# Differential attention: PV sums moved into spare columns of a lasting score tile, one PSUM bank handed to the projections, and one minimum taken by a single reduce

## The chip, the core and the metric

The kernel runs on one core of one Trainium2 chip. The metric is the device time of one execution in microseconds (us), as a median of several runs. Five engines work side by side and wait for each other through semaphores: TensorE (PE, matrix multiplies, whose weight loads are shown apart as PEld), VectorE (DVE), ScalarE (ACT), GpSimd (POOL) and SyncE (SP), which issues most of the DMAs. Each engine takes its instructions in the order in which they stand.

## What is computed

A block of two layers works on 2048 latent tokens and 256 context tokens of width 1024. Each layer normalises the tokens, multiplies them with one wide projection matrix, feeds four groups of heads from it (differential attention, HGRN2, windowed attention, mLSTM), gates their joined output, and projects it back. The change lies in differential attention, which has four heads:

```python
def attend(qs, ks, vs):                      # qs, ks: two maps (m) per head, 32 wide; vs: 64 wide
    s = jnp.einsum('mbhqd,mbhkd->mbhqk', qs, ks).astype(F32) * scale
    p = jax.nn.softmax(s, axis=-1)
    w = (p[0] - lam * p[1]).astype(vs.dtype)
    return jnp.einsum('bhqk,bhkv->bhqv', w, vs)
...
y = from_heads(rmsnorm(o, g) * (1.0 - lam_init))
```

Each query row has two maps of scores against all 2304 keys. Both are turned into softmax weights, the second is subtracted with the factor lam, and the difference is multiplied with the values ("PV" below).

## The kernel before

In each layer there is first a stage that normalises and transposes the tokens and makes the projections that differential attention needs. Then comes the **diff loop**, in which differential attention runs while all the other projections are worked off in its gaps. After it the windowed attention, mLSTM, HGRN2 and output streams are woven together.

The diff loop walks over **units**. A unit is one head and one tile of 128 queries: 64 units with latent queries in each layer, and 8 with context queries in layer 0 alone. For a latent unit the 2304 keys are cut into two halves (HALF): 1024 keys and 1280 keys. Keys are in fp16 as a high and a low part, and so are the values and the weights. For a unit u the steps are these:

- diff_scores(u, m) makes the scores of one map. PE writes the first half into the tile sc0 (1024 columns, two matmuls of 512), then works off some projections (`pump(FSTEP)`), then writes the second half into sc1 (1536 columns reserved, 1280 used, three matmuls). DVE takes a minimum over each half (L1048). A last small instruction joins the two minima into the bias of the exponential: L1054, a tensor_tensor, for map 1, and L1056, a tensor_scalar, for map 0.
- diff_exp(u, m) is the exponential of each half on ACT, read straight from sc0 and sc1.
- diff_mix(u, j) subtracts the maps on DVE (L1082), splits the difference into two fp16 parts on ACT (L1084) and POOL (L1085), and has a DMA transpose it into wt (L1087).
- diff_out(u, j) is PV of half j on PE. For each block of 128 keys there are two matmuls: the high weights with the high and low part of the values (128 columns) and the low weights with the high part (64 columns). Both halves add up in one tile pv.
- diff_norm(u, 0) copies one half of pv, scaled, to ot on ACT, and diff_norm(u, 1) adds the other half to it on DVE (oall, L1120).

Four units are in flight: while u makes scores, u1, u2 and u3 are the three before it. The order of one round is written out by hand, and it is PE's order word for word; the other engines' order is set by a scheduler at build time:

```python
diff_scores(u, 1); diff_out(u3, 1); pump(FGAP); diff_mix(u1, 0); diff_exp(u, 1); diff_norm(u3, 0)
diff_scores(u, 0); diff_norm(u3, 1); diff_out(u2, 0); pump(FGAP); diff_mix(u1, 1); diff_exp(u, 0)
```

So on PE a PV burst stands right behind the three matmuls of sc1, and projections (`pump(FGAP)`) stand behind the burst. A round has two such **map steps**: sc0, projections, sc1, a PV burst, projections.

The matmuls' output memory, PSUM, is dealt out in pools that add up to eight banks of 512 fp32 columns: in the diff loop two for sc0, three for sc1, one for pv and two for the projections (pool pps, tag "pp"). After the diff loop, while projections are left, windowed attention has three, mLSTM three (function bank, GPB = 4) and the projections two; when they are done, bank also draws from a second pool.

The tiles' waits are placed by the framework that builds the program, from what each instruction reads and writes. The small tile sm holds a unit's minima, sums and biases; u["nm"] is the joining instruction behind which diff_mix is issued. All matmuls but the transposes are recorded in a helper at L94, the activations at L105, the tensor_tensor operations at L108 and the fused DVE operations at L111.

Of the kernel before, what the change touches and what calls it, by code (L numbers as in the profile page):

```python
# [10 lines left out]
F32 = mybir.dt.float32  # L11
# [3 lines left out]
AF = mybir.ActivationFunctionType  # L15
ALU = mybir.AluOpType
# [57 lines left out]
def kernel(  # L74
# [29 lines left out]
    def act(o, i, f, **kw):  # L104
        A.activation(out=o, in_=i, func=f, **kw)  # L105

    def tt(e, o, a, b, op):
        return e.tensor_tensor(out=o, in0=a, in1=b, op=op)  # L108
# [150 lines left out]
    for l in range(n_layers):  # L259
# [79 lines left out]
            hl[g] = hp.tile([P, KC, GROUPS[g][1]], F16, tag=f"hl{g}", name=f"hl{l}_{g}")  # L339
        wst = ExitStack()  # L340
        wp = wst.enter_context(tc.tile_pool(name=f"wp{l}", bufs=1, reuse_waits="tile"))
        pps = wst.enter_context(tc.tile_pool(name=f"pps{l}", bufs=2, reuse_waits="tile", space=PSUM))
        with tc.tile_pool(name=f"pa{l}", bufs=2, reuse_waits="tile", side="right" if l else "left") as pa, tc.tile_pool(name=f"pap{l}", bufs=4, space=PSUM, reuse_waits="tile") as pap:
            xgs = {}

# [682 lines left out]
        with ExitStack() as st2:  # L1028
            da = st2.enter_context(tc.tile_pool(name=f"da{l}", bufs=2, reuse_waits="tile", side="right"))
            sps = st2.enter_context(tc.tile_pool(name=f"sps{l}", bufs=1, reuse_waits="tile", space=PSUM, side="right"))  # L1030
            HALF = [(0, 1024), (1024, 1280)]

            def halves_of(u):
                return [(2048, 256)] if u["ctx"] else HALF

            def diff_scores(u, m):


                sm, hs = u["sm"], halves_of(u)
                pss = u["s", m] = []  # L1040
                for j, (k0, n) in enumerate(hs):
                    ps = sps.tile([P, 1536 if j else 1024], F32, tag=f"sc{j}", name="scr")
                    for o in range(0, n, 512):
                        w = min(512, n - o)
                        mm(ps[:, o:o + w], u["Qs"][:, m, u["qo"]:u["qo"] + P], u["Ks"][m][:, k0 + o:k0 + o + w], True, True)
                    if j < len(hs) - 1:
                        pump(FSTEP * u["work"])
                    V.tensor_reduce(sm[:, m * 2 + j:m * 2 + j + 1], ps[:, :n], AX.X, ALU.min)  # L1048
                    pss.append(ps)
                o = m * 2  # L1050
                o2 = o + len(hs) - 1

                if m:
                    u["nm"] = tt(V, sm[:, 5:6], sm[:, o:o + 1], sm[:, o2:o2 + 1], ALU.min)  # L1054
                else:
                    u["nm"] = V.tensor_scalar(sm[:, 4:5], sm[:, o:o + 1], sm[:, o2:o2 + 1], shf, ALU.min, ALU.add)  # L1056

# [32 lines left out]
            def diff_out(u, j):  # L1090

                sm, hs = u["sm"], halves_of(u)
                if j >= len(hs):
                    return
                if u["start"]:
                    h = u["h"]
                    k0_, n_ = HALF[j]
                    head["V", j] = da.tile([P, n_ // P, P], F16, tag=f"Vs{j}", name=f"Vs{h}", bufs=1)
                    SP.dma_start(head["V", j], dva[k0_:k0_ + n_, h].rearrange("(t p) c -> p t c", p=P))
                if j == 0:  # L1100
                    u["pv"] = sps.tile([P, 512], F32, tag="pv", name="pv")
                pv, wt = u["pv"], u["w"][j]
                nb = hs[j][1] // P
                vv = head["V", 1][:, 8:] if u["ctx"] else head["V", j]
                fin = j == len(hs) - 1
                for b in range(nb):
                    mm(pv[:, 0:P], wt[:, b], vv[:, b], j == 0 and b == 0, False)
                    mm(pv[:, 0:64], wt[:, nb + b], vv[:, b, 0:64], False, fin and b == nb - 1)

            def diff_norm(u, j):  # L1110
                sm, pv = u["sm"], u["pv"]
                if j == 0:
                    ot = u["ot"] = da.tile([P, 64], F32, tag="ot", name="ot")
                    act(ot, pv[:, 64:128], AF.Copy, scale=sm[:, 12:13])
                    return
                ot, (i, nq) = u["ot"], u["of"]
                if i == 0:
                    head["o"] = da.tile([P, 8, 64], F32, tag="oall", name="oall")
                oall = head["o"]
                stt(oall[:, i], pv[:, 0:64], sm[:, 12:13], ot, ALU.mult, ALU.add)  # L1120
                if i == nq - 1:
                    h, q0 = u["h"], u["qt"] + 1 - nq
                    rs = da.tile([P, 2, 8], F32, tag="rs", name=f"drs{h}")
# [9 lines left out]
            def units():  # L1133
                for h in range(4):
# [5 lines left out]
                    for g in ([0, 1, 4, 2, 3] if cq else [0, 1, 2, 3]):  # L1140
# [5 lines left out]
                        for i in range(n // P):  # L1146
                            qt = g0 // P + i
                            ctx_ = qt >= NL
                            yield dict(h=h, qt=qt, Ks=Ks, Qs=Qs, qo=i * P, ctx=ctx_, start=qt == 0,
                                       work=CTXW if ctx_ else 1.0, of=(i, 2) if ctx_ else (qt % 8, 8),  # L1150
                                       sm=da.tile([P, 16], F32, tag="sm", name="sm", bufs=5))

            owed = [0.0]

            def pump(ns):
                owed[0] += ns
# [42 lines left out]
        with ExitStack() as st4:  # L1201
# [10 lines left out]

            def bank(shape, name):
                turn_[0] += 1
                if gps2 and turn_[0] % GPB == 0:
                    return gps2.tile(shape, F32, tag="gp", name=name)
                return gps.tile(shape, F32, tag="gp", name=name, bufs=GPB - 1)

            def yt_of(i):

# [506 lines left out]
```

## Time and profile before

| | |
|---|---|
| median of 3 runs | 4207.11 us (4199.64 to 4225.74) |
| the profiled execution | 4225.03 us, its span 4223.2 us |
| PE busy | 3576.0 us, 85% |
| DVE busy | 2834.6 us, 67% |
| ACT busy | 2333.8 us, 55% |
| POOL busy | 2355.6 us, 56% |

The profile is of one execution, whose span lies 2 us under its own time and 0.4% above the median. Busy times are shares of the whole span; the change touches two stretches of it, the diff loops of the two layers, and these are read by themselves below. In the rows, a name with "<-" is what is written and what is read, x is a count, and what stands in brackets is how long the engine sat idle before the instruction and what released it.

### The profile page before, as it was taken

The numbers are of one execution on the slowest core, as the hardware profiler recorded it, in microseconds if no ns is written. First come the engines' busy times: TensorE is split into PE (matmuls) and PEld (weight loads), VectorE is DVE, ScalarE is ACT, GpSimd is POOL, SyncE is SP. The second block draws the span as 40 slices with busy tenths as digits, with TensorE's granted clock in tenths as the row PEclk, the third lists the DMA queues.
The fourth block names the chain that finished last, engine by engine and source line by source line (L and its number), as shares of the span: only waits on it lengthen the run. The fifth ranks groups of instructions, "written<-read, shape, count | busy, mean of one in ns | idle before, by whom it ended". The sixth has DMA issues, their size and how long they took to land. (4 is left out here: it accounts for less than half of the span.)

```text
span 4223.2 us, 78658 instructions
## 1 busy us (share of the span) xinstructions
PE 3576.0 (85%) x30342; PEld 2404.5 (57%) x30342; DVE 2834.6 (67%) x4343; ACT 2333.8 (55%) x4679; POOL 2355.6 (56%) x1727
## 2 busy tenths in 40 slices
PE   6988878888769986999989887787877798789998
PEld 3656645444547675666657475544454565556665
DVE  5167888889894546556543599888898665555654
ACT  4245656666655545566643366566666565545553
POOL 4443555443445457788757446645334554777763
PEclk9999989999989986889899999999998899678879
DMA  5356856667656546578644467577775662655762
GB/s 204 99 139 151 192 127 164 134 149 157 128 141 163 136 137 145 153 191 190 175 145 139 119 138 153 128 151 154 151 158 126 164 150 92 171 130 147 174 148 78
DMA packets 1256959, 622.19 MB, mean 147 GB/s; under 512 B 913476, under 2 KB 1203848, under 8 KB 1256584
## 3 DMA queue, kind: packets, MB, share of 16 engines
q1 hardware_dynamic: 1154216, 490.64, 51.4%
q10 hardware_dynamic: 102368, 126.52, 9.0%
q8 instruction: 239, 3.92, 0.4%
q14 instruction: 136, 1.11, 0.1%
HBM read 291.76 MB, written 131.23 MB: 100 GB/s over the span
## 5 line engine op out<-in xcount | busy, mean ns | idle before, releaser
L108 POOL TENSOR_TENSOR p<-p,p 128x1024 f16<-128x1024 f32 (+2 forms) x264 | 627.3, 2377 | 786.4 <-ACT p L1084 706.4
L94 PE MATMUL ptm<-wb,hh 128*128 128x256 f16 (+2 forms) x5024 | 839.4, 274 | 31.1 <-DVE dSs L111 8.1
L105 ACT ACTIVATE p<-scr,sm 128x1024 f32<-128x1024 f32 (+2 forms) x528 | 628.0, 1193 | 422.7 <-DVE sm L1073 143.8
L1048 DVE TENSOR_REDUCE sm<-scr 128x1 f32<-128x1024 f32 (+2 forms) x528 | 698.9, 1326 | 214.8 <-PE scr L94 210.9
L94 PE MATMUL pfm<-hh,wb 128*128 128x512 f16 (+1 forms) x2592 | 803.4, 374 | 29.8 <-DVE gz L111 10.2
L94 PE MATMUL ptm<-wb,hl 128*128 128x256 f16 (+2 forms) x2512 | 674.1, 274 | 2.1 <-POOL hl L108 2.1
L94 PEld LDWEIGHTS <-wb 128*128 128x128 f16 x3888 | 376.2, 100 | 407.2 <-issue 72.6
L94 PE MATMUL scr<-Ks,Qs 128*128 128x512 f16 (+1 forms) x1296 | 362.3, 379 | 282.1 <-ACT p L105 279.4
L94 PEld LDWEIGHTS <-hh 128*128 128x128 f16 x5024 | 481.5, 100 | 134.7 <-issue 37.8
L94 PE MATMUL pfm<-hl,wb 128*128 128x512 f16 (+1 forms) x1296 | 484.4, 374 | 0.0
L111 DVE SCALAR_TENSOR_TENSOR p<-p,sm,p 128x1024 f32<-128x1024 f32 (+2 forms) x264 | 414.3, 1570 | 8.1
L94 PE MATMUL fx<-wo,mh 128*128 128x512 f16 x1088 | 370.0, 424 | 7.9 <-DVE yt L108 4.8
L94 PEld LDWEIGHTS <-Qs 128*128 128x128 f16 x1296 | 130.5, 102 | 422.7 <-issue 352.2
L1084 ACT CAST p<-p 128x1024 f16<-128x1024 f32 (+2 forms) x264 | 297.5, 1127 | 40.6 <-DVE p L111 35.4
L94 PEld LDWEIGHTS <-wt 128*128 128x128 f16 x4640 | 239.6, 101 | 80.0 <-DMA wt<-p 27.5
L94 PE MATMUL pv<-Vs,wt 128*128 128x128 f16 (+1 forms) x4640 | 254.1, 212 | 30.4 <-DMA wt<-p 16.4
L94 PEld LDWEIGHTS <-hl 128*128 128x128 f16 x2512 | 251.7, 100 | 35.9 <-POOL hl L108 3.5
L108 POOL TENSOR_TENSOR E<-lk,cm 128x512 f32<-128x512 f32 (+1 forms) x136 | 203.0, 1493 | 49.8 <-PE gA L94 24.7
L94 PE MATMUL fx<-wo,mlo 128*128 128x512 f16 x544 | 228.7, 420 | 1.5 <-DVE mlo L108 1.3
L108 POOL TENSOR_TENSOR ph<-swp,ph 128x640 f16<-128x640 f32 (+2 forms) x136 | 190.2, 1399 | 49.5 <-ACT ph L1326 36.6
L108 DVE TENSOR_TENSOR QQ<-hq,E 128x512 f32<-128x512 f32 x119 | 152.3, 1289 | 90.6 <-ACT E L105 38.2
L105 ACT ACTIVATE E<-E 128x1024 f32<-128x1024 f32 x136 | 143.1, 1052 | 82.7 <-POOL E L108 73.6
(298 smaller groups left out, 6835.2 us busy)
## 6 DMA issues: line engine op xcount, KB each, us to landing
wraw<-in_w_in_dram SPq DMA_DIRECT2D x60, 512.0 KB
dgt<-ga ACTq DMA_DIRECT2D x68, 256.0 KB
r1b<-dr SPq DMA_DIRECT2D x68, 256.0 KB
gtt<-dgt SPq DMA_DIRECT2D x34, 512.0 KB
mraw<-in_w_mod_dram SPq DMA_DIRECT2D x64, 256.0 KB
vi<-dhi SPq DMA_DIRECT2D x49, 256.0 KB
KSb<-dsk SPq DMA_DIRECT2D x56, 192.0 KB
Ks<-dka SPq DMA_DIRECT2D x64, 144.0 KB
```

The source lines that it names most:

```text
L94: PE.matmul(o, lhsT=lhsT, rhs=rhs, start=start, stop=stop)
L105: A.activation(out=o, in_=i, func=f, **kw)
L108: return e.tensor_tensor(out=o, in0=a, in1=b, op=op)
L111: V.scalar_tensor_tensor(out=o, in0=a, scalar=s, in1=b, op0=op0, op1=op1)
L1048: V.tensor_reduce(sm[:, m * 2 + j:m * 2 + j + 1], ps[:, :n], AX.X, ALU.min)
L1084: A.copy(wl[:, :n], p[:, :n])
```

## The change

There are three edits, and what follows from them. The tile pv goes away. In its place sc1 is allocated once for the whole diff loop and PV sums are written into its last 256 columns, which no score uses, in four slots of 64 columns: two for the halves of one unit, in turn for units with even and odd number. The matmul of 128 columns becomes two of 64 that add to the same slot, so a block of keys has three matmuls and three weight loads where it had two. The bank of pv goes to the pool pps, which has three now; since that pool lives on into the next stage, bank has two instead of three there until the projections are done. And the joined minimum of map 1 is taken by one tensor_reduce over two neighbouring columns of sm. diff_norm reads slot 0 on ACT and slot 1 on DVE; a context unit has one slot alone, which ACT writes to oall.

```diff
-        pps = wst.enter_context(tc.tile_pool(name=f"pps{l}", bufs=2, reuse_waits="tile", space=PSUM))
+        pps = wst.enter_context(tc.tile_pool(name=f"pps{l}", bufs=3, reuse_waits="tile", space=PSUM))
...
             HALF = [(0, 1024), (1024, 1280)]
+            sc1 = sps.tile([P, 1536], F32, tag="sc1", name="scr1")
...
-                    ps = sps.tile([P, 1536 if j else 1024], F32, tag=f"sc{j}", name="scr")
+                    ps = sc1 if j else sps.tile([P, 1024], F32, tag="sc0", name="scr")
...
                 if m:
-                    u["nm"] = tt(V, sm[:, 5:6], sm[:, o:o + 1], sm[:, o2:o2 + 1], ALU.min)
+                    u["nm"] = V.tensor_reduce(sm[:, 5:6], sm[:, o:o2 + 1], AX.X, ALU.min)
...
-                if j == 0:
-                    u["pv"] = sps.tile([P, 512], F32, tag="pv", name="pv")
-                pv, wt = u["pv"], u["w"][j]
+                pv = sc1[:, 1280 + (u["n"] % 2 * 2 + j) * 64:][:, :64]
+                u["pv", j], wt = pv, u["w"][j]
...
                 for b in range(nb):
-                    mm(pv[:, 0:P], wt[:, b], vv[:, b], j == 0 and b == 0, False)
-                    mm(pv[:, 0:64], wt[:, nb + b], vv[:, b, 0:64], False, fin and b == nb - 1)
+                    mm(pv, wt[:, b], vv[:, b, 0:64], b == 0, False)
+                    mm(pv, wt[:, b], vv[:, b, 64:128], False, False)
+                    mm(pv, wt[:, nb + b], vv[:, b, 0:64], False, b == nb - 1)
...
-                sm, pv = u["sm"], u["pv"]
+                rz = u["sm"][:, 12:13]
                 if j == 0:
-                    ot = u["ot"] = da.tile([P, 64], F32, tag="ot", name="ot")
-                    act(ot, pv[:, 64:128], AF.Copy, scale=sm[:, 12:13])
+                    if not u["ctx"]:
+                        u["ot"] = da.tile([P, 64], F32, tag="ot", name="ot")
+                        act(u["ot"], u["pv", 0], AF.Copy, scale=rz)
                     return
...
-                stt(oall[:, i], pv[:, 0:64], sm[:, 12:13], ot, ALU.mult, ALU.add)
+                if u["ctx"]:
+                    act(oall[:, i], u["pv", 0], AF.Copy, scale=rz)
+                else:
+                    stt(oall[:, i], u["pv", 1], rz, u["ot"], ALU.mult, ALU.add)
...
-                if gps2 and turn_[0] % GPB == 0:
-                    return gps2.tile(shape, F32, tag="gp", name=name)
-                return gps.tile(shape, F32, tag="gp", name=name, bufs=GPB - 1)
+                if gps2 and turn_[0] % GPB >= 2:
+                    return gps2.tile(shape, F32, tag="gp", name=name, bufs=GPB - 2)
+                return gps.tile(shape, F32, tag="gp", name=name, bufs=2)
```

How the built program's instructions stand is shown at two places. A bracket names the semaphores of the engines for which an instruction waits. The first place is PE in an early round of layer 0, where the last score matmul of map 1 is followed by the PV burst of an older unit's second half. Before:

```order
L94 MATMUL scr<-Ks_1_2087,Qs_1_2666 128x256
L94 LDWEIGHTS wt [waits DMAHW2_49]
L94 MATMUL pv<-Vs_2527,wt 128x128
L94 LDWEIGHTS wt
L94 MATMUL pv<-Vs_2527,wt 128x64
L94 LDWEIGHTS wt
L94 MATMUL pv<-Vs_2527,wt 128x128
```

The same place now, where scr_2084 is the lasting tile sc1 and scr without a number is sc0:

```order
L94 MATMUL scr_2084<-Ks_1_2088,Qs_1_2683 128x256
L94 LDWEIGHTS wt [waits DMAHW2_49]
L94 MATMUL scr_2084<-Vs_2528,wt 128x64 [waits DVE_49]
L94 LDWEIGHTS wt
L94 MATMUL scr_2084<-Vs_2528,wt 128x64
L94 LDWEIGHTS wt
L94 MATMUL scr_2084<-Vs_2528,wt 128x64
L94 LDWEIGHTS wt
L94 MATMUL scr_2084<-Vs_2528,wt 128x64
```

The burst's first matmul carries a wait for DVE that it did not carry; in the built program the count that it waits for is that of DVE's minimum over the sc1 just written (L1049), although the columns differ, and in bursts of a first half it is that of oall, which now stands behind that minimum.

The second place is DVE between one map 1 and the following map 0. Before, from oall of an older unit over the joined minimum of map 1 (L108) and the mixing to the two minima of map 0 (L1048) and theirs joined (L1056):

```order
L111 SCALAR_TENSOR_TENSOR oall<-pv,sm,ot 128x64 [waits Activation_49]
L108 TENSOR_TENSOR sm<-sm 128x1 [waits DVE_49]
L1073 TENSOR_REDUCE sm<-sm 128x2
L1074 RECIPROCAL sm<-sm 128x2 [waits DVE_49]
L1075 TENSOR_SCALAR sm<-sm,nlam_122 128x1 [waits DVE_49]
L111 SCALAR_TENSOR_TENSOR p_5172<-p_5172,sm,p_5284 128x1024 [waits DVE_49,Pool_49]
L1048 TENSOR_REDUCE sm<-scr 128x1 [waits PE_49] x2
L1056 TENSOR_SCALAR sm<-sm,shf_123 128x1 [waits DVE_49]
```

Now, the corresponding rows of a round nearby (the projection's row tm is DVE work that happens to stand there):

```order
L1055 TENSOR_REDUCE sm<-sm 128x1 [waits DVE_49]
L1074 TENSOR_REDUCE sm<-sm 128x2
L1075 RECIPROCAL sm<-sm 128x2 [waits DVE_49]
L1076 TENSOR_SCALAR sm<-sm,nlam_122 128x1 [waits DVE_49]
L111 SCALAR_TENSOR_TENSOR p_5130<-p_5130,sm,p_5237 128x1024 [waits DVE_49,Pool_49]
L111 SCALAR_TENSOR_TENSOR tm<-ptm,bg 128x256 [waits PE_49]
L1049 TENSOR_REDUCE sm<-scr 128x1 [waits PE_49]
L1049 TENSOR_REDUCE sm<-scr_2084 128x1 [waits PE_49,Activation_49]
L111 SCALAR_TENSOR_TENSOR oall<-scr_2084,sm,ot 128x64
L1057 TENSOR_SCALAR sm<-sm,shf_123 128x1 [waits DVE_49]
```

The row oall has moved from ahead of map 1's joined minimum to behind both minima of map 0, since it reads the tile that map 0's scores are written to.

## Rows read from the trace of the kernel before

**Rows 1.** The page: span, and busy time of each engine.

```profile
span 4223.2 us, 78658 instructions
PE 3576.0 (85%) x30342; PEld 2404.5 (57%) x30342; DVE 2834.6 (67%) x4343; ACT 2333.8 (55%) x4679; POOL 2355.6 (56%) x1727
```

**Rows 2.** Busy time by stretch, both diff loops: length, engines, granted clock, DMA.

```profile
236.90:1252.00 1015.10, 810.78 (x7111) 532.89 (x7110) 849.49 (x1242) 597.48 (x982) 454.56 (x261) 0.94 0.66 149
2373.50:3292.00 918.50, 728.53 (x6385) 479.11 (x6383) 810.41 (x1128) 573.54 (x892) 447.46 (x245) 0.95 0.66 142
```

**Rows 3.** Timeline, one step of map 1 in layer 0: start, length.

```profile
1016.46 0.70 PE L94 MATMUL scr<-Ks,Qs 128*128 128x512 f16 x3
1017.00 1.01 PE L94 MATMUL pv<-Vs,wt 128*128 128x128 f16 x20
1017.20 1.49 DVE L1048 TENSOR_REDUCE sm<-scr 128x1 f32<-128x1280 f32 x1 [0.61 <-PE scr L94]
1017.22 2.62 POOL L108 TENSOR_TENSOR p<-p,p 128x1280 f16<-128x1280 f32 x1 [3.27 <-ACT p L1084]
...
1017.85 0.38 PE L94 MATMUL pfm<-hh,wb 128*128 128x512 f16 x1
...
1018.80 1.05 DVE L108 TENSOR_TENSOR sm<-sm 128x1 f32<-128x1 f32 x1
...
1019.94 1.11 ACT L105 ACTIVATE p<-scr,sm 128x1024 f32<-128x1024 f32 x1 [0.56 <-DVE sm L1073]
...
1020.22 0.38 PE L94 MATMUL pfm<-hh,wb 128*128 128x512 f16 x1
...
1021.05 1.32 ACT L105 ACTIVATE p<-scr,sm 128x1280 f32<-128x1280 f32 x1
1021.20 0.59 PE L94 MATMUL scr<-Ks,Qs 128*128 128x512 f16 x2 [0.60 <-ACT p L105]
```

**Rows 4.** Who waited for whom, PE: us in total, times, longest us.

```profile
PE scr L94 <- ACT p L105: 279.4, 198, 7.3
PE mdc L94 <- DVE dCs L111: 22.4, 9, 5.7
PE pv L94 <- DMA wt<-p: 16.4, 11, 3.6
PE pv L94 <- DVE oall L111: 14.0, 6, 6.0
PE pfm L94 <- DVE gz L111: 10.2, 6, 4.5
```

**Rows 5.** Groups by line and shape: count, busy us, mean ns, idle before.

```profile
L1048 DVE TENSOR_REDUCE sm<-scr 128x1 f32<-128x1280 f32 x256 | 381.0, 1488 | 117.5 <-PE scr L94 116.9
L94 PE MATMUL pv<-Vs,wt 128*128 128x128 f16 x2320 | 246.0, 226 | 30.4 <-DMA wt<-p 16.4 <-DVE oall L111 14.0
L108 DVE TENSOR_TENSOR sm<-sm 128x1 f32<-128x1 f32 x136 | 101.0, 743 | 0.6
L111 DVE SCALAR_TENSOR_TENSOR oall<-pv,sm,ot 128x64 f32<-128x64 f32 x136 | 37.4, 275 | 12.0 <-ACT ot L105 12.0
L1073 DVE TENSOR_REDUCE sm<-sm 128x2 f32<-128x4 f32 (+1 forms) x136 | 19.8, 146 | 0.9 <-ACT p L105 0.9
```

**Rows 6.** Timeline, PE, matmuls of 128 columns in layer 0.

```profile
432.11 0.27 PE L94 MATMUL ptm<-wb,hh 128*128 128x128 f16 x2
432.22 0.22 PE L94 MATMUL ptm<-wb,hl 128*128 128x128 f16 x1
432.27 0.27 PE L94 MATMUL ptm<-wb,hh 128*128 128x128 f16 x2
```

**Rows 7.** Timeline, PE, the sc0 matmuls of consecutive map steps in layer 1.

```profile
3013.93 0.59 PE L94 MATMUL scr<-Ks,Qs 128*128 128x512 f16 x2 [0.34 <-ACT p L105]
...
3019.49 0.59 PE L94 MATMUL scr<-Ks,Qs 128*128 128x512 f16 x2
...
3025.95 0.59 PE L94 MATMUL scr<-Ks,Qs 128*128 128x512 f16 x2 [1.24 <-ACT p L105]
```

More of the change, by code (lines that the diff above doesn't have):

```diff
@@ L1099, in diff_out @@
                     SP.dma_start(head["V", j], dva[k0_:k0_ + n_, h].rearrange("(t p) c -> p t c", p=P))
-                if j == 0:
-                    u["pv"] = sps.tile([P, 512], F32, tag="pv", name="pv")
-                pv, wt = u["pv"], u["w"][j]
+                pv = sc1[:, 1280 + (u["n"] % 2 * 2 + j) * 64:][:, :64]
+                u["pv", j], wt = pv, u["w"][j]
                 nb = hs[j][1] // P
                 vv = head["V", 1][:, 8:] if u["ctx"] else head["V", j]
-                fin = j == len(hs) - 1
                 for b in range(nb):
-                    mm(pv[:, 0:P], wt[:, b], vv[:, b], j == 0 and b == 0, False)
-                    mm(pv[:, 0:64], wt[:, nb + b], vv[:, b, 0:64], False, fin and b == nb - 1)
+                    mm(pv, wt[:, b], vv[:, b, 0:64], b == 0, False)
+                    mm(pv, wt[:, b], vv[:, b, 64:128], False, False)
+                    mm(pv, wt[:, nb + b], vv[:, b, 0:64], False, b == nb - 1)
             def diff_norm(u, j):
-                sm, pv = u["sm"], u["pv"]
+                rz = u["sm"][:, 12:13]
                 if j == 0:
-                    ot = u["ot"] = da.tile([P, 64], F32, tag="ot", name="ot")
-                    act(ot, pv[:, 64:128], AF.Copy, scale=sm[:, 12:13])
+                    if not u["ctx"]:
+                        u["ot"] = da.tile([P, 64], F32, tag="ot", name="ot")
+                        act(u["ot"], u["pv", 0], AF.Copy, scale=rz)
                     return
-                ot, (i, nq) = u["ot"], u["of"]
+                i, nq = u["of"]
                 if i == 0:
@@ L1148, in units @@
                             ctx_ = qt >= NL
-                            yield dict(h=h, qt=qt, Ks=Ks, Qs=Qs, qo=i * P, ctx=ctx_, start=qt == 0,
+                            n_units[0] += 1
+                            yield dict(h=h, qt=qt, n=n_units[0], Ks=Ks, Qs=Qs, qo=i * P, ctx=ctx_, start=qt == 0,
                                        work=CTXW if ctx_ else 1.0, of=(i, 2) if ctx_ else (qt % 8, 8),
                                        sm=da.tile([P, 16], F32, tag="sm", name="sm", bufs=5))
-            owed = [0.0]
+            owed, n_units = [0.0], [0]
             def pump(ns):
```

## Prediction

> **What bounds the kernel now.** I read the page first: PE is busy for 85% of the span, no other engine for more than 67% [rows 1]. That is a mean over stages, and nearly everything that the change moves lies in the two diff loops, so I read those by windows next [rows 2]: 1015.10 and 918.50 us, together 1933.6. In them PE is busy for 810.78 + 728.53 = 1539 us and DVE for 849.49 + 810.41 = 1660, which is 84 and 88%. Neither is full. Both run in a loop of waits, and the timeline of one map step shows it [rows 3]. PE ends the scores of sc1 and starts the PV burst at 1017.00. DVE takes its minimum over sc1 from 1017.20 to 1018.69. PE meanwhile has gone on with the burst and from 1017.85 with projections. DVE joins the minima (1018.80, 1.05 us), ACT takes the exponential of sc0 (1019.94, 1.11 us), and only then may PE write sc0 again, at 1021.20, after 0.60 us idle and 0.15 us after ACT's end. So two paths run side by side from the end of sc1: DVE and ACT, 4.2 us here, and PE's own burst and projections, 3.6 us. They are nearly equal. The table of waits says the same for the whole kernel: PE waited 279.4 us for ACT to give back a score tile, 198 times, at most 7.3 us, for 272 maps [rows 4]. PE hides its work behind the minimum and the exponential almost exactly. What matters is what may run beside what.
>
> **The wait that the change adds.** In the built program the burst's first matmul now waits for DVE's minimum over the sc1 just written, or, in bursts of a first half, for oall directly behind that minimum. Before, the burst ran beside this minimum [rows 3]: 1017.00 against 1017.20 to 1018.69. Now it starts at 1018.69 plus the 0.15 us that PE took after ACT's release, 1018.84, which is 1.84 us later. PE takes its matmuls in order, so the projections behind the burst and the next sc0 are late by as much; DVE waits for that sc0, and DVE and ACT for the projections' results. How many bursts: a layer has 64 latent units with two map steps, less 5 at the start where u2 and u3 are still missing, less 8 in layer 0 because a context unit has no second half: 115 + 123 = 238. The minimum lasts 1488 ns in the mean of 256 [rows 5], so this step is typical and not a late one. 238 x 1.84 = **438 us** of new idle time on PE. If PE were released at once it would be 402; where DVE reaches the minimum late, more.
>
> This row speaks of two tiles that were separate before, and it cannot show that the wait must be. The Trainium skill does, in "PSUM — Partial Sum Buffer", section "PSUM bank collisions raise a hardware error": two engines may not be in the same bank and the same 32 partitions at the same time, whatever the columns, and waits have to be set by bank. By that rule the spare columns of sc1 are no free place for a sum while its scores are being read; by columns alone there would be no wait, and the sum below would come to about zero.
>
> **What of it is covered.** PE already idles at the end of the same step, and that idle time vanishes first. In the step above it was 0.60 of the 1.84, so the step grows by 1.24. Three steps in a row of layer 1 show 0.34, none and 1.24 us [rows 7], a mean of 0.53, which over 238 steps is 125 us. All of it would be 279 and, with the projections' own waits of which the largest are 22.4 and 10.2 [rows 4] and which I put at 60 together as an estimate from them, 340. A step cannot use more than its own wait, and part of the 279 sits in a few long ones of up to 7.3 us. I take three quarters of the 279: **-210 us**, between -125 and -340.
>
> **oall.** It moves behind the minima of map 0, and the bursts of first halves wait for it too: 62 in each layer, 124 x 0.275 us [rows 5] = **+35**, between 0 (if it runs while PE waits anyway) and 35.
>
> **PV in three matmuls.** A block took one matmul of 128 and one of 64 columns. The 20 of the step above run from 1017.00 to 1017.85, so 85 ns a block [rows 3]. Matmuls of 128 columns follow each other at (432.27 - 432.11) / 3, about 55 ns [rows 6], which leaves about 29 for one of 64. Three of them are 87: 2320 blocks [rows 5] x 2 ns = **+5 us**. Should every matmul, with its weight load, need the burst's mean of 42.5 ns, it is 2320 x 42.5 = 98. I take the lower end, since in the burst a matmul of 64 columns is followed 29 ns later with a weight load for each.
>
> **Map 1's joined minimum.** The tensor_tensor takes 743 ns for one column, the reduce of sm that stands nearest 146 [rows 5]. In the step above it ended at 1019.85, just when POOL's operation of 2.62 us from 1017.22 did [rows 3]. At 128 latent units that is 128 x 0.6 = 76 us off the DVE and ACT path. But that path is no longer the last: from the minimum's end at 1018.69, DVE and ACT would have sc0 free 1.5 us later, and PE comes for it after 0.15 + 0.85 + 2.6 = 3.6 us. So the gain is covered by PE's own late work; it would be worth 76 if PE were not late. I take **-10**, for steps in which DVE is late.
>
> **ACT.** The exponential of sc1 reads the bank that PV writes and waits for the burst's end, about 1 us behind the minimum. It stands behind the joined minimum and the exponential of sc0, 1.3 us together, so nothing: cover is 0.3 us, and it would be gone if the burst took 1.3 us. ot now needs only the older slot, which is earlier than before; ACT is busy for 1171 of 1934 us [rows 2], so that buys nothing.
>
> **Banks and queues.** The third projection bank can save at most the projections' waits for their results, whose rows are small [rows 4]: **-15**, between -60 and 0, and much of that is in the absorbed part already. mLSTM with two banks while projections last: **+5**, 0 to 20, from the same small rows. The transposes on SP wait for the burst that frees their tile; a late burst delays them and the loads behind them by 2 us in a round of 14, and they are needed a round later: nothing. That wait for pv's single buffer, 14.0 us [rows 4], is inside the new one.
>
> **Clock.** Granted were 0.94 and 0.95 of full speed in these stretches [rows 2]. More idle time on PE may lower it. I take **+15**, between 0 and 77, which is what 0.05 less on 1539 us of PE work would cost.
>
> **Sum.** 438 - 210 + 35 + 5 - 10 - 15 + 5 + 15 = **+263 us** on the profiled execution of 4225.03, so 4488. That execution is 0.4% over the median, so against the median of 4207.11 it is **4470 us**, 6.2% slower.
>
> **Rivals.** (1) *The stall is free and the kernel gets faster.* Then the DVE and ACT path stays the last one, the wait lies wholly beside it, and the short reduce takes its 76 us off: 4207 - 76, about 4130. It decides where wait, burst and projections together, 1.84 + 0.85 + 2.6 = 5.3 us, are shorter than that path, 4.2 us before and 3.6 after. For it speaks that DVE is busy for 84 to 88%; against it, that projections behind the burst would have to last under 0.9 us. (2) *Nearly everything is absorbed*, because DVE's late minima are what PE's idle time really stands for, and PE late means DVE caught up: 438 + 35 - 340 - 25 = 108, about 4315. For it: the longest waits of 7.3 us cannot come from one minimum and one exponential. Against it: the steps of rows 7 idle far less than 1.84. (3) *Worse:* little is absorbed (125), the matmuls of 64 columns are paced by their loads (98) and the clock falls (77): 438 - 125 + 35 + 98 + 77 = 523, about 4730. For it: the regular new gap in PE's work. Against it: the 29 ns in today's burst. (4) *The freed bank does nothing.* Its rows are so small that this moves the sum by 15 and is in the range.
>
> **How the numbers follow.** Forecast 0.72; rival 1 0.07; rival 2 0.12; rival 3 0.09. The forecast's own range, with absorption between 125 and 300, is 4370 to 4570. For eight in ten I add rival 2 and the lower part of rival 3: 4310 to 4610. A measurement of this kernel tells about 1% from nothing. Faster by over 1%: rival 1, 0.07. Within 1%: what rival 2 leaves under 4250, 0.04. Slower: 0.89.
>
> **What would show it.** In the new profile the first PV matmul of a burst sits idle before it by 1.5 to 2 us and is released by DVE's minimum or oall, 238 times, 400 to 480 us in all; PE's wait for ACT before sc0 falls from 279 to under 100; DVE's wait for PE's scores grows by the difference; the two loops last about 1150 and 1045 us instead of 1015 and 919, and the rest of the kernel keeps its length within 20 us; the reduce at the place of L1054 takes about 0.15 us; a burst of 30 matmuls lasts about 0.87 us. The prediction is wrong if the bursts show no idle time, or if it is there and PE's other idle time falls by as much.

## The result and the profile after

The changed kernel takes 4433.15 us in the median of 4 runs (4431.09 to 4439.13), beside 4203.38 us for the kernel before (4 runs, 4192.92 to 4225.74). The ratio is 1.0542, with a 95% interval of 1.0497 to 1.0586: slower by 230 us.

The page of the changed kernel, span and busy time; PE has fallen from 85% to 81% [rows 1] while its busy time has grown by 28 us, so what was added is idle time:

```profile
span 4429.3 us, 83627 instructions
PE 3604.4 (81%) x32662; PEld 2430.0 (55%) x32662; DVE 2732.0 (62%) x4335; ACT 2328.3 (53%) x4679; POOL 2358.7 (53%) x1727
```

The windows of the two diff loops of the changed kernel (bounds, length, busy time of PE, PEld, DVE, ACT, POOL, granted clock, DMA share, GB/s), cut again at the first and last score matmul of each layer:

```profile
233.60:1345.00 1111.40, 826.84 (x8167) 545.02 (x8166) 793.00 (x1231) 595.27 (x981) 455.95 (x260) 0.93 0.62 136
2470.00:3508.00 1038.00, 742.06 (x7438) 491.51 (x7437) 760.07 (x1125) 567.08 (x889) 443.09 (x243) 0.93 0.61 125
```

Beside [rows 2], the loops last 2149.4 us instead of 1933.6: 96 us more in layer 0 and 120 in layer 1, together 216. The spans differ by 206, so the rest of the kernel has become some 10 us shorter. PE's busy time in the loops is 1568.9 for 1539.3, so it is idle there for 580.5 us instead of 394.3: 186 us more idle and 30 us more work.

PE's waits in the changed kernel (us in total, times, longest us) say where the idle time has moved:

```profile
PE scr L94 <- DVE oall L111: 253.1, 115, 8.3
PE scr L94 <- DVE sm L1049: 249.1, 116, 9.7
PE scr L94 <- ACT p L105: 33.5, 25, 4.7
```

The two rows on top did not exist before. Both are PV bursts, now written into a tile named scr: the 116 of second halves wait for DVE's minimum (L1049), the 115 of first halves for oall, which stands behind that minimum. Together 502 us at 231 bursts. The wait for ACT ahead of the scores, the largest of before at 279.4 [rows 4], has shrunk to 33.5.

Groups by shape in the changed kernel (count, busy us, mean ns, idle before and its releasers):

```profile
L1049 DVE TENSOR_REDUCE sm<-scr 128x1 f32<-128x1280 f32 x256 | 380.9, 1488 | 85.9 <-PE scr L94 82.0 <-ACT sp L530 1.4 <-ACT p L1085 0.7
L94 PE MATMUL scr<-Vs,wt 128*128 128x64 f16 x6960 | 271.5, 200 | 540.7 <-DVE oall L111 253.1 <-DVE sm L1049 249.1 <-ACT oall L105 16.7
L94 PE MATMUL scr<-Ks,Qs 128*128 128x512 f16 x1024 | 310.5, 385 | 36.9 <-ACT p L105 33.5 <-ACT ot L105 3.2
L94 PE MATMUL pfm<-hh,wb 128*128 128x512 f16 x2176 | 743.0, 401 | 0.9 <-ACT fm L105 0.9
L94 PE MATMUL ptm<-wb,hh 128*128 128x256 f16 x3872 | 686.6, 282 | 10.1 <-DVE tm L111 4.5 <-ACT wb L105 2.6 <-DVE dSs L111 2.1
L94 PE MATMUL mdc<-mv,kw 128*64 128x65 f32 x576 | 27.9, 242 | 0.0
L1055 DVE TENSOR_REDUCE sm<-sm 128x1 f32<-128x2 f32 x128 | 19.5, 153 | 3.4
```

The kernel before has these rows for the four of PE's groups that lost idle time (the last column again):

```profile
L94 PE MATMUL scr<-Ks,Qs 128*128 128x512 f16 x1024 | 327.0, 403 | 276.6 <-ACT p L105 273.9 <-DMA dhi<-tm 0.2
L94 PE MATMUL pfm<-hh,wb 128*128 128x512 f16 x2176 | 727.8, 392 | 26.5 <-DVE gz L111 7.1 <-ACT rp L105 6.2 <-ACT kT L722 4.8
L94 PE MATMUL ptm<-wb,hh 128*128 128x256 f16 x3872 | 680.6, 280 | 22.7 <-DVE dSs L111 8.1 <-DVE tm L111 4.5 <-DMA xg<-xh 2.8
L94 PE MATMUL mdc<-mv,kw 128*64 128x65 f32 x576 | 27.7, 240 | 28.8 <-DVE dCs L111 22.4 <-DVE sm L1074 5.9 <-DVE gz L111 0.6
```

This is the balance of the change. The bursts' idle time was 30.4 [rows 5] and is 540.7: 510 us new. PE's idle time in the loops grew by 186 alone, so 324 us were covered. The four groups show 307 of them: 240 ahead of the scores, 26 and 13 at the projections, 29 at mdc, which is mLSTM's. With 30 us more work, 510 - 324 + 30 = 216 us, which is what the loops grew by.

The timeline of the changed kernel in layer 0 (start, length, engine, line, operation, count; in brackets the idle time before it and its releaser), from the end of one map 1 step through the next map step, with the scores and the burst that follow:

```profile
997.35 1.22 DVE L1049 TENSOR_REDUCE sm<-scr 128x1 f32<-128x1024 f32 x1
...
998.58 1.49 DVE L1049 TENSOR_REDUCE sm<-scr 128x1 f32<-128x1280 f32 x1
1000.10 0.16 DVE L1055 TENSOR_REDUCE sm<-sm 128x1 f32<-128x2 f32 x1
1000.12 1.03 PE L94 MATMUL scr<-Vs,wt 128*128 128x64 f16 x30 [2.40 <-DVE sm L1049]
1000.37 1.11 ACT L105 ACTIVATE p<-scr,sm 128x1024 f32<-128x1024 f32 x1 [5.86 <-DVE sm L1074]
1001.08 0.51 PE L94 MATMUL mdc<-mv,kw 128*64 128x65 f32 x8
...
1005.05 0.59 PE L94 MATMUL scr<-Ks,Qs 128*128 128x512 f16 x2
...
1006.78 0.70 PE L94 MATMUL scr<-Ks,Qs 128*128 128x512 f16 x3
...
1007.59 1.49 DVE L1049 TENSOR_REDUCE sm<-scr 128x1 f32<-128x1280 f32 x1 [0.68 <-PE scr L94]
1009.00 0.28 DVE L111 SCALAR_TENSOR_TENSOR oall<-scr,sm,ot 128x64 f32<-128x64 f32 x1
1009.33 0.86 PE L94 MATMUL scr<-Vs,wt 128*128 128x64 f16 x24 [1.84 <-DVE oall L111]
...
1012.44 0.59 PE L94 MATMUL scr<-Ks,Qs 128*128 128x512 f16 x2
...
1015.87 1.03 PE L94 MATMUL scr<-Vs,wt 128*128 128x64 f16 x30 [1.65 <-DVE sm L1049]
```

In [rows 3] the burst starts before the minimum does. Here it starts at 1000.12, 0.05 us after the minimum's end at 1000.07, and the next one at 1009.33, 0.05 us after the end of oall. Behind each, the scores of sc0 in the following step come without a wait: 1005.05 and 1012.44 have no bracket.

Such bursts are not all alike. Taken one by one from the trace, the middle one of the 116 that wait for the minimum idles for 1.65 us, as the last row does, and the middle one of the 115 that wait for oall for 1.84, as the row at 1009.33 does. The means, 2.15 and 2.20, are higher by those in which DVE is late, as at 1000.12.

### The profile page after: what moved, and what is told of

Its sections match the earlier page's. It is cut to its first block, busy times and chain, and to the rows that moved or that the text cites. A ratio compares the mean times of both kernels' runs of the same rounds, so it can differ in the third digit from the quotient of the medians.

```text
span 4429.3 us, 83627 instructions
## 1 busy us (share of the span) xinstructions
PE 3604.4 (81%) x32662; PEld 2430.0 (55%) x32662; DVE 2732.0 (62%) x4335; ACT 2328.3 (53%) x4679; POOL 2358.7 (53%) x1727
## 5 line engine op out<-in xcount | busy, mean ns | idle before, releaser
L108 POOL TENSOR_TENSOR p<-p,p 128x1024 f16<-128x1024 f32 (+2 forms) x264 | 620.6, 2351 | 1000.0 <-ACT p L1085 901.0
L1049 DVE TENSOR_REDUCE sm<-scr 128x1 f32<-128x1024 f32 (+2 forms) x528 | 699.6, 1327 | 430.7 <-PE scr L94 425.6
L94 PE MATMUL ptm<-wb,hh 128*128 128x256 f16 (+2 forms) x5024 | 854.9, 277 | 10.1 <-DVE tm L111 4.5
L94 PE MATMUL pfm<-hh,wb 128*128 128x512 f16 (+1 forms) x2592 | 822.1, 383 | 1.2 <-ACT fm L105 0.9
L94 PE MATMUL scr<-Vs,wt 128*128 128x64 f16 x6960 | 271.5, 200 | 540.7 <-DVE oall L111 253.1
L94 PEld LDWEIGHTS <-wb 128*128 128x128 f16 x3888 | 386.9, 103 | 396.9 <-issue 74.0
L94 PEld LDWEIGHTS <-wt 128*128 128x128 f16 x6960 | 262.4, 103 | 616.2 <-issue 576.3
L94 PE MATMUL pfm<-hl,wb 128*128 128x512 f16 (+1 forms) x1296 | 496.8, 383 | 0.0
L94 PE MATMUL scr<-Ks,Qs 128*128 128x512 f16 (+1 forms) x1296 | 343.4, 362 | 36.9 <-ACT p L105 33.5
L108 POOL TENSOR_TENSOR E<-lk,cm 128x512 f32<-128x512 f32 (+1 forms) x136 | 203.1, 1494 | 49.8 <-PE gA L94 23.2
L108 POOL TENSOR_TENSOR ph<-swp,ph 128x640 f16<-128x640 f32 (+2 forms) x136 | 192.5, 1416 | 49.4 <-ACT ph L1331 44.9
L108 DVE TENSOR_TENSOR QQ<-hq,E 128x512 f32<-128x512 f32 x119 | 147.9, 1250 | 84.4 <-ACT E L105 50.4
```

The lines of the kernel that those rows point to most:

```text
L94: PE.matmul(o, lhsT=lhsT, rhs=rhs, start=start, stop=stop)
```

## The experiments

The change has four parts: PV sums live in the tile whose scores are being read, a block has three matmuls, the joined minimum is a reduce, and a bank moves to the projections. The theory of the prediction is that the first makes the loss through the wait of the burst; its rivals are that one of the other three makes it. Beside that stands the question of why the wait is there at all: because of the bank or because of the tile. All ratios are to the kernel before on the same chip.

**The slots in a tile of their own.** The rest of the change stays, but for the bank, which this needs: projections and mLSTM have their banks of before.

```diff
             sc1 = sps.tile([P, 1536], F32, tag="sc1", name="scr1")
+            pvs = sps.tile([P, 512], F32, tag="pv", name="pv")
...
-                pv = sc1[:, 1280 + (u["n"] % 2 * 2 + j) * 64:][:, :64]
+                pv = pvs[:, (u["n"] % 2 * 2 + j) * 64:][:, :64]
```

> The changed kernel with the four PV slots in a PSUM bank of their own instead of in the spare columns of sc1, and so with two projection banks and mLSTM's three banks as before; the three matmuls a block, the lasting sc1, the reduce for map 1 and the slots stay. Theory (the burst waits because it shares a bank with scores that DVE still reads): the bursts' idle time falls from 502 us to under 40, PE's wait for ACT before sc0 comes back to some 200 us, and the time is 4130 to 4205 us, 0.983 to 1.000 of before. Rival A (the third matmul and weight load of each block cost it): the time stays near 4430, 1.05 of before. Rival B (the lasting sc1 tile costs it, whatever is put into it): the time stays near 4430 too, with idle time before the sc1 scores.

Measured: 4159.7 us, ratio 0.989 (0.9859 to 0.9921). PE's waits and its burst in this kernel:

```profile
PE scr L94 <- ACT p L105: 261.9, 171, 7.5
```

```profile
L94 PE MATMUL pv<-Vs,wt 128*128 128x64 f16 x6960 | 264.0, 198 | 18.9 <-DMA wt<-p 13.7 <-DVE oall L111 5.3
```

With the slots elsewhere the bursts idle 18.9 us instead of 540.7, the wait for ACT is back at 262, and the loss has turned into a gain of 1.1%. The same 6960 matmuls and the same reduce are still there, so neither of them makes the loss. The bank that went to the projections is not it either: in the next kernel they are without it too, and that one is slow.

**The same tile, another bank.** Now sc1 is widened to four banks and the slots lie in the fourth, which no score touches: the difference to the kernel above is only that the slots belong to the tile that DVE reads.

```diff
-            sc1 = sps.tile([P, 1536], F32, tag="sc1", name="scr1")
-            pvs = sps.tile([P, 512], F32, tag="pv", name="pv")
+            sc1 = sps.tile([P, 2048], F32, tag="sc1", name="scr1")
...
-                pv = pvs[:, (u["n"] % 2 * 2 + j) * 64:][:, :64]
+                pv = sc1[:, 1536 + (u["n"] % 2 * 2 + j) * 64:][:, :64]
```

> The run own_bank with the slots once more inside the lasting sc1, which is made 2048 columns wide, so that they lie in the same tile as the scores but in its fourth bank, which no score touches. Theory (it is the bank): the same as own_bank, 0.989 of before within 0.005, idle time ahead of the bursts under 40 us. Rival (it is the tile: waits are set for a tile as a whole): the idle time of 502 us and the 4430 us of the changed kernel are back.

Measured: 4439.18 us, ratio 1.0559 (1.0533 to 1.0585). PE's waits:

```profile
PE scr L94 <- DVE sm L1049: 250.4, 116, 9.5
PE scr L94 <- DVE oall L111: 242.3, 114, 6.3
...
PE scr L94 <- ACT p L105: 35.6, 26, 4.9
```

These are the rows of the changed kernel to within 11 us, although the slots share no bank with the scores any more. A common tile is enough for the wait, without a common bank. The two kernels differ by 279 us (1.0559 beside 0.989), which is the price of this wait with nothing else changed: 493 us in the two rows of the bursts, less the 226 that the wait for ACT loses (261.9 to 35.6), with smaller differences in other waits and in PE's work, which were not added up.

**The matmuls alone.** The kernel before with three matmuls of 64 columns in a block.

```diff
-                    mm(pv[:, 0:P], wt[:, b], vv[:, b], j == 0 and b == 0, False)
+                    mm(pv[:, 0:64], wt[:, b], vv[:, b, 0:64], j == 0 and b == 0, False)
+                    mm(pv[:, 64:128], wt[:, b], vv[:, b, 64:128], False, False)
```

> The kernel before with the matmul of 128 columns of PV in two of 64 that go to the two halves of pv, each with a weight load; nothing else. The prediction's price of 2 ns a block: 5 us, 1.001 of before, and a burst of 30 matmuls in 0.87 us. Its upper bound (each matmul takes the old burst's mean of 42.5 ns): a burst of 30 in 1.28 us and up to 98 us, 1.01 to 1.02. Rival A of the run own_bank asks for 1.05.

Measured: 4195.17 us, ratio 0.9984 (0.9964 to 1.0005): nothing. The bursts' group in this kernel:

```profile
L94 PE MATMUL pv<-Vs,wt 128*128 128x64 f16 x6960 | 258.4, 196 | 21.9 <-DMA wt<-p 14.3 <-DVE oall L111 7.6
```

In the kernel before, the matmuls of 128 columns [rows 5] overlap with those of 64, since matmuls are pipelined; what both cover together is the window over the whole span with PE's work on the tile pv alone (length, busy time, count, granted clock, DMA share, GB/s):

```profile
0.00:4300.00 4300.00, 254.08 (x4640) 0.90 0.60 145
```

2320 more matmuls and weight loads are 4 us more, beside a forecast of 5 and a bound of 98. From the first matmul of a burst to the one behind it, the middle burst of a second half has gone from 849 to 874 ns for ten blocks, 2.5 ns a block.

**The reduce alone.** The kernel before, and of the change only this:

```diff
-                    u["nm"] = tt(V, sm[:, 5:6], sm[:, o:o + 1], sm[:, o2:o2 + 1], ALU.min)
+                    u["nm"] = V.tensor_reduce(sm[:, 5:6], sm[:, o:o2 + 1], AX.X, ALU.min)
```

> The kernel before with map 1's joined minimum taken by one reduce and nothing else changed. If DVE and ACT are the last path in a good part of the map steps, as the prediction reads the kernel before: 0.15 us instead of 0.74 for 128 instructions, PE's wait for ACT before sc0 falls from 279 to 200 to 240 us, and the time falls by 20 to 60 us, to about 0.990 of before. Rival (the two paths are so equal that PE takes over at once): 1.000 within 0.003.

Measured: 4136.46 us, ratio 0.9834 (0.9801 to 0.9867), the fastest of all kernels here. Its group:

```profile
L1054 DVE TENSOR_REDUCE sm<-sm 128x1 f32<-128x2 f32 x128 | 18.4, 144 | 0.3
```

743 ns have become 144 [rows 5], so 128 x 0.6 = 77 us left DVE's path. The kernel is shorter by 67, by the interval 56 to 84, where 20 to 60 were expected. PE's wait for ACT ahead of the scores is 245.7 us, just outside the 200 to 240 expected. From first to last score matmul, the two loops of the profiled execution are 43 us shorter (1885.9 for 1928.7); where the rest of the 67 came off is not shown.

**The changed kernel with the old joined minimum**, the same line turned back.

> The changed kernel with the old tensor_tensor for map 1's joined minimum. The prediction holds that the short reduce is worth 10 us once PE is the late path: 4433 to 4450 us, 1.055 to 1.060 of before, with the instruction back at 0.5 to 0.9 us. Rival (it is worth in the changed kernel what it is worth in the kernel before, 67 us): about 4500, 1.070.

Measured: 4419.52 us, ratio 1.0519 (1.0489 to 1.0549), no different from the change as it is. One row of its waits and one of its groups:

```profile
PE scr L94 <- DVE oall L111: 255.7, 115, 8.2
```

```profile
L108 DVE TENSOR_TENSOR sm<-sm 128x1 f32<-128x1 f32 x136 | 52.6, 387 | 3.6
```

The tensor_tensor itself has become shorter without being touched: 387 ns for 743, so no more than 128 x 0.23 = 30 us was at stake here. Even of these nothing shows in the time, which fits that PE comes late and the path through the joined minimum is no longer the last one. The loops are 6 us longer than in the changed kernel (2151.2 for 2145.6, from first to last score matmul), which single executions don't tell from nothing: among the kernels here with a short joined minimum and no new wait for DVE, the loops differ by 14 us.

**The changed kernel with two projection banks** (the pool pps back to bufs=2).

> The changed kernel with two projection banks instead of three, so that the freed bank lies idle. The prediction's price of the third bank is 15 us, between 0 and 60: 1.054 to 1.068 of before, with the projections' waits for their results back at some 20 to 40 us. Rival (the third bank takes a good part of the new wait away again): 1.075 or more.

Measured: 4421.13 us, ratio 1.0513 (1.0485 to 1.0541). Its bursts wait as before:

```profile
PE scr L94 <- DVE sm L1049: 252.8, 116, 10.1
PE scr L94 <- DVE oall L111: 245.9, 115, 6.3
```

The interval overlaps with that of the change, so in the time the third bank buys nothing that can be told. Idle time does come back where it was expected: the two groups of projections shown above for the changed kernel idle for 17.8 and 24.8 us instead of 0.9 and 10.1. The loops are 11 us longer (2156.9 for 2145.6), near the 15 of the prediction, but no more than single executions differ by.

**The burst moved behind the projections.** The changed kernel, with diff_out and pump exchanged in both steps of a round, so that projections fill the time of the minimum:

```diff
+                    pump(FGAP * (u["work"] if u else 1.0))
                     if u3:
                         diff_out(u3, 1)
-                    pump(FGAP * (u["work"] if u else 1.0))
```

> The changed kernel with each PV burst behind the projections of its map step instead of ahead of them, so that PE has work while DVE takes its minimum over sc1; all else as in the changed kernel. Theory: the wait is still in the program but is over when PE comes to it; the bursts' idle time falls from 502 to under 80 us and the time to 4130 to 4210, 0.985 to 1.002 of before. Rival (the exponential of sc1 reads the same bank and must now wait for a burst that is 2.6 us later, and sc0 of the next map waits for ACT behind it): ACT waits 0.5 to 1 us in each of 238 steps, and the time is 4250 to 4350.

Measured: 4167.75 us, ratio 0.9925 (0.99 to 0.995). PE's waits and the bursts' group:

```profile
PE scr L94 <- ACT p L105: 227.3, 191, 5.8
...
PE scr L94 <- ACT ot L105: 49.3, 48, 7.1
PE scr L94 <- DVE oall L111: 43.9, 20, 7.7
...
PE scr L94 <- DVE sm L1049: 18.9, 11, 4.7
```

```profile
L94 PE MATMUL scr<-Vs,wt 128*128 128x64 f16 x6960 | 251.7, 195 | 79.1 <-DVE oall L111 43.9 <-DVE sm L1049 18.9 <-ACT oall L105 4.8
```

The shared tile can be kept if PE has other work while DVE reads it: 540.7 us at the bursts become 79.1. What is left is the tile again: scores of sc1 wait 49.3 us for ACT's copy out of a slot (ot), in another place of the same tile.

**The late burst without the shared tile.** The kernel before with the reduce and the bursts behind pump.

> The kernel before with the reduce for map 1 and each PV burst behind the projections of its map step; pv keeps its own bank. It tells what late_burst lacks against reduce_only (0.9925 against 0.9834). If the late place of the burst is what costs (ot and oall come later, and sc1 and the next burst wait for them), this is about 0.990, with PE waiting for ot or oall. If it is the shared bank, this is 0.983 within 0.004.

Measured: 4149.69 us, ratio 0.9868 (0.9849 to 0.9886). Two rows of its waits:

```profile
PE scr L94 <- ACT p L105: 255.7, 191, 6.2
...
PE pv L94 <- DVE oall L111: 13.7, 8, 2.7
```

The late place costs 0.3% beside the reduce alone, which is less than the intervals tell apart, and its loops are no longer (1872.2 us for 1885.9). The kernel above it has the shared tile, the three matmuls and the third bank besides, and is half a per cent slower; its loops last 1897.5 us, 25 more. The three matmuls show no such cost in the last experiment below, and the waits for ot and oall point to the tile, but the parts were not separated.

**Another form of the joined minimum.** The kernel before, with the minimum as a tensor_scalar, which reads one column as its tensor and the other as a scalar per partition. It asks whether the reduce or the going of the tensor_tensor makes the gain.

```diff
-                    u["nm"] = tt(V, sm[:, 5:6], sm[:, o:o + 1], sm[:, o2:o2 + 1], ALU.min)
+                    u["nm"] = V.tensor_scalar(sm[:, 5:6], sm[:, o:o + 1], sm[:, o2:o2 + 1], None, ALU.min)
```

> The kernel before with map 1's joined minimum taken by a tensor_scalar whose second operand is a pointer scalar, the form that map 0 uses, instead of the tensor_tensor; nothing else. Theory (the tensor_tensor is long because it waits until POOL's tensor_tensor ends, and any form that does not would do): 0.26 to 0.28 us for the instruction and 0.983 to 0.990 of before. Rival (the gain of reduce_only is the reduce's own shortness): the instruction is as long as the tensor_tensor, or the gain is under a third of 1.7%.

Measured: 4147.09 us, ratio 0.9875 (0.9843 to 0.9907). Its group:

```profile
L1054 DVE TENSOR_SCALAR sm<-sm 128x1 f32<-128x1 f32 x136 | 27.8, 204 | 0.6
```

A form of another kind takes 204 ns, less than the 260 to 280 expected, and gives most of the gain. It is the tensor_tensor that was dear.

**The reduce and the three matmuls.** The remaining half per cent between the slots in their own tile (0.989) and the reduce alone (0.9834) is looked for here: the kernel before with both of these edits.

> The kernel before with two parts of the change at once: map 1's joined minimum by a tensor_reduce, and PV as three matmuls of 64 columns into the old pv tile. It asks where the half per cent lies between reduce_only (0.9834) and own_bank (0.989). Theory A (the third matmul costs something once DVE's short join has made PE the later path): the ratio comes near 0.988, PE's wait for ACT ahead of the scores stays near 246 us and PE's busy time in the bursts grows by 10 to 20 us. Theory B (the half per cent lies in the lasting score tile, the slots or ot): the ratio stays near 0.983, as three matmuls without the reduce measured 0.9984.

Measured: 4149.12 us, ratio 0.9895 (0.9858 to 0.9932). The ratio is the one that the first theory asks for. Of its rows, the wait for ACT near 246 us is too, PE's work in the bursts is not:

```profile
PE scr L94 <- ACT p L105: 251.9, 168, 6.4
```

```profile
L94 PE MATMUL pv<-Vs,wt 128*128 128x64 f16 x6960 | 257.1, 196 | 23.7 <-DMA wt<-p 13.8 <-DVE oall L111 8.0 <-DVE gates L638 1.9
```

PE is busy with PV for 257.1 us, where 10 to 20 more than before's 254.1 were expected. (This number is no fine measure: in the reduce alone, the 4640 matmuls of before cover 261.6 us in the same view.) Its span (4143.4 us) lies 7.5 us above that of the reduce alone (4135.9), and the intervals of the two ratios overlap between 0.9858 and 0.9867. That the third matmul costs half a per cent once the join is short would fit the ratio, but the loops, where its work lies, speak against it: from first to last score matmul they last 1885.9 us with the reduce alone, 1882.5 here and 1883.7 with the slots in their own tile. What the spans of the three differ by lies outside the loops, where none of these edits stands. So neither theory is borne out, and the half per cent stays open; it may be no more than the spread of single executions and medians.

## Why the prediction was right, and what in it was wrong

The time, 4433 us, lies 37 us under the 4470 of the prediction and inside its range, and what it named as signs is there in kind: bursts released by the minimum and by oall, the wait for ACT ahead of the scores under 100 us (33.5), the loops at 1111 and 1038 us where 1150 and 1045 were expected, the rest within 20 us, the reduce at 0.153 us, the middle burst of 30 matmuls at 0.87. Its sizes for the wait were missed: 502 us where 400 to 480 were named, at 231 bursts instead of 238. DVE pays with a longer wait for scores, as expected; the row of the waits of all engines in the kernel before and in the changed one:

```profile
DVE sm L1048 <- PE scr L94: 210.9, 255, 6.9
DVE sm L1049 <- PE scr L94: 425.6, 327, 4.6
```

That is 215 us more, about as much as the loops grew by.

**The wait: right in kind, and near in size by luck.** 238 bursts of 1.84 us and 35 us for oall made 473; 510 us are measured, 502 of them at 231 bursts (115 + 116), 2.17 us each. The prediction had said that more would come where DVE reaches the minimum late, and the timeline has such a burst: the one at 1000.12 has PE idle from 997.72, and DVE begins the minimum only at 998.58, since until 998.57 it is busy with that over sc0. In [rows 3] it begins 0.74 us after PE begins the last scores and 0.20 after PE is ready for the burst; here it is 0.86 after that. But the regular part was taken too large. PE starts 0.05 us behind the minimum, where 0.15 was taken from ACT's release, and DVE mostly begins 0.11 us after PE is ready, where rows 3 show 0.20: 0.11 + 1.49 + 0.05 = 1.65 us instead of 1.84. oall ends 0.19 us behind the minimum in the middle one of its bursts, as in the timeline (1009.08 and 1009.28): 22 us at 115 bursts instead of 35. At their middle lengths the 231 bursts would idle for 116 x 1.65 + 115 x 1.84 = 403 us; the other 99 of the 502 come from late minima, which the sum did not price. Two errors cancel.

**What is covered: right in kind, mis-sized.** This is the step that failed in size. 210 us were forecast, between 125 and 340, with 15 for the third bank and 10 for the joined minimum besides: 235 in all, and 324 are measured. The term took three quarters of the wait for ACT; 246 of 279 went (88%). The 60 us put on the own waits of the projections and mdc were right, 67 of them show in three groups, but the sum had counted few of them. With 89 us more covered, 37 more of new idle time, 30 instead of 25 for matmuls, mLSTM and clock, and 10 less outside the loops, the 263 us of the sum become the 206 by which the spans differ. The medians differ by 230, because the profiled execution of before, 4225.03 us, lies 22 above its median. Those 22 seem to lie outside the loops: with three matmuls and nothing else changed the loops last as long as before (1928.8 beside 1928.7 us, from first to last score matmul), and the rest is 28 us shorter. So the time came 37 us under the forecast by errors of both signs, of which the largest is the absorption.

**PV: right.** 5 us were forecast, 4 came in the kernel that has this edit alone. The upper bound of 98, matmuls paced by their loads, is ruled out. In the changed kernel the bursts' busy time is 17 us above before, and PE's in the loops 30 above where 20 were forecast for matmuls and clock; the granted clock went from 0.94 and 0.95 to 0.93. Of the 17, about 10 go with the clock: 43 of the 256 bursts of latent units take over 1.1 times the middle length, where 28 did before. In all of them the granted clock is at the lower of its two levels (1.2 GHz) at their start or end. What all bursts take beyond the middle length has grown from 12.8 to 23.3 us. How the remaining 13 of the 30 split was not separated. That the sum's price was so near owes something to rounding: rows 6 give 53 ns rather than 55, and with 53 the same sum makes a block some 10 ns longer, 23 us in all.

**The joined minimum: right.** It would be worth 76 if PE were not late: 67 without the wait (the reduce alone), and nothing that the time shows with it (the old form put back: 1.0519 beside 1.0542). The two can't be set side by side in full, since the old form is only 387 ns long there. The 10 us that were taken for it in the sum are less than the intervals tell apart.

**The third bank: not to be told in the time.** 15 us were forecast; the projections' idle time and the loops move by about that (32 and 11 us), the median does not. Whether rival 4 was the better guess stays open, and it moves the sum by little, as it said.

**The reason for the wait: not the one that the runs show.** The prediction put it down to the bank that scores and sums share. That a wait is there was read from the built program, and the sum stood on that; but the slots in a bank of their own wait for 493 us as long as they belong to the same tile, and for 5 us behind DVE when they don't. The rule of the Trainium skill, in "PSUM — Partial Sum Buffer", section "PSUM bank collisions raise a hardware error", that waits are to be set by bank, may hold all the same: two tiles in one bank were not tried, and no run here shows it. What decided in this kernel is the unit in which the framework sets waits. Whoever had followed the bank alone would have moved the slots to a free bank of the same tile and kept the loss.

**Rivals.** The stall was not free (rival 1): the path of PE with wait, burst and projections is the later one, as the vanished wait for ACT shows. Rival 2 had the absorption nearly right (340 forecast, 324 measured), but the new idle time was larger than its 473, and its further 25 us for the reduce and the bank did not come. Rival 3 needed little absorption and slow matmuls; neither came.

## What to carry to other kernels

Columns of a tile that nothing uses are no free place when waits are set for whole tiles: what has to run beside a read of a tile belongs into another tile, or behind other work that fills the read (540.7 us became 79.1 that way). Where two engines' paths are nearly equal, an edit on one is worth what it says only while that path is the later one; the same reduce gave 67 us without the new wait and nothing that the time shows with it. So parts of a change are timed one by one: here the part that looked smallest, one line, is a gain of 1.7% (0.9834, 0.9801 to 0.9867) and alone beats both kernels, and the rest of the change buried it.

## What the hardware showed that was not expected

A tensor_tensor of one column took 743 ns in the mean [rows 5], and in the step of [rows 3] it ended at 1019.85, as POOL's tensor_tensor of 2.62 us did at 1019.84. Two forms that read a single tensor in its place took 144 and 204 ns, and the same tensor_tensor took 387 where the other parts of the change stood around it. Two more places of the kernel before, one with POOL at work and one without:

```profile
950.87 2.61 POOL L108 TENSOR_TENSOR p<-p,p 128x1280 f16<-128x1280 f32 x1 [3.71 <-ACT p L1084]
952.04 1.46 DVE L108 TENSOR_TENSOR sm<-sm 128x1 f32<-128x1 f32 x1
...
1008.04 0.16 DVE L108 TENSOR_TENSOR sm<-sm 128x1 f32<-128x1 f32 x1
```

Counted over all 136 in that trace, 93 begin while an instruction of POOL of over 0.3 us runs: they take 1.02 us in the mean, and 90 of them end within 0.04 us of its end. The other 43 take 0.15 us. With the old form put back into the changed kernel, 42 of the 136 begin so, which is why they are shorter there; the reduce and the tensor_scalar take the same time either way. So the tensor_tensor is held until POOL's instruction ends. Removing 128 of them brought 67 us of 4200. The Trainium skill says in "SBUF — State Buffer", section "Who interferes with whom", that a DVE instruction with two inputs in SBUF contends with a GpSimd instruction that reads SBUF, while a tensor_reduce on trn2 never does. The trace agrees: 743 beside 144 ns, and 1.02 us beside 0.15 with and without POOL at work.
